# A rotation of 96 images by 90 degrees: the last 2 MB of loads in transfers of 48, 16 and 64 partitions instead of 64 and 64, and the first store released by the first of them

## The chip, the core and the metric

The kernel runs on one core of a Trainium2 chip. The metric is the device time of one execution in microseconds (us). Before the change it was 122.96 us, the median of 3 runs (122.85 to 123.09).

## What is computed

The input x is a float32 array of shape 32 x 3 x 256 x 256, 96 images of 256 x 256 and 25.17 MB in all. Each image is turned clockwise by 90 degrees:

```
def reference(x):
    return np.rot90(x, k=-1, axes=(-2, -1)).astype(np.float32)
```

So `out[.., i, j] = x[.., 255 - j, i]`. Nothing is added or multiplied. Each of the 25.17 MB is read from HBM once and written to HBM once, and between the two the elements change places on the chip.

## The kernel before, in words

**Tiling.** The 24,576 image rows are taken as 1,536 pieces of 16 rows (`R = 16`). A piece is 16 rows x 256 columns x 4 bytes = 16 KB and lies contiguously in HBM. Twelve pieces fall to each of the 128 partitions. They are cut into five groups (`sizes = (2, 2, 2, 4, 2)`, line 38), and each group has a tile of its own, `u0` to `u4`, with 2 or 4 pieces per partition. All twelve pieces of a partition are on the chip at once (192 KB), so no buffer is used a second time and no load waits for a buffer.

**Loads (lines 52 to 66).** All are issued by SyncE (SP). Group 0 comes in two transfers of 1 MB (line 55) and one of 2 MB (line 56). Groups 1 to 4 come in `I` = 2 or 4 transfers each (line 66): transfer `i` fills every `I`-th partition, starting at partition `i`. In groups 1, 2 and 4 this is 64 partitions with two pieces of 16 KB each, 2 MB per transfer. The last transfer of the last group is an exception (lines 62 to 64). It is cut by slot: line 63 loads slot 0 of partitions 1, 3, ..., 127 (64 pieces, 1 MB), and line 64 loads slot 1 of the same partitions (1 MB). Line 63's transfer is called `mark`.

**Turning (lines 68 to 101).** VectorE (DVE) does the turning with transposes of 32 x 32 blocks, 128 x 2048 elements per instruction. Since a transpose writes where another one has yet to read, one quarter or half of each group is parked in `spare` (in PSUM) or in `extra`, and ScalarE (ACT) copies it to its place afterwards (lines 78 and 98).

**Stores (lines 104 to 113).** They are issued by SP too, two per group, each from every second partition (`groups[n][a::2]`): eight of 2 MB and two of 4 MB (group 3). A store waits for the DVE and ACT instructions of its group. The very first store of group 0 (line 106, `a == 0`) has one dependency more, written by hand in lines 107 to 109: it waits until `mark` has landed. As SP issues in order, all the other stores stand behind it.

**What sets the order.** SP is one in-order queue: 14 loads, then 10 stores. The framework gives each DMA one of eight completion semaphores in turn. A DMA therefore waits, ahead of its issue, until the DMA eight places before it has landed, since both use the same semaphore. All transfers go through one DMA queue, which feeds the core's 16 DMA engines.

The list of transfers, with their places in SP's order:

| places | line | what | size of each |
|---|---|---|---|
| 0, 1 | 55 | group 0, slot 0 | 1 MB |
| 2 | 56 | group 0, slot 1 | 2 MB |
| 3 to 6 | 66 | groups 1 and 2 | 2 MB |
| 7 to 10 | 66 | group 3 | 2 MB |
| 11 | 66 | group 4, even partitions | 2 MB |
| 12 | 63 | group 4, odd partitions, slot 0 (`mark`) | 1 MB |
| 13 | 64 | group 4, odd partitions, slot 1 | 1 MB |
| 14, 15 | 106 | stores of group 0 | 2 MB |
| 16 to 19 | 113 | stores of groups 1 and 2 | 2 MB |
| 20, 21 | 113 | stores of group 3 | 4 MB |
| 22, 23 | 113 | stores of group 4 | 2 MB |

Of the kernel before, what the change touches and what calls it, by code (L numbers as in the profile page):

```python
# [1 line left out]

# [4 lines left out]


@with_exitstack  # L10
def kernel(
    ctx: ExitStack,
    tc: tile.TileContext,
    x: bass.AP,
    out: bass.AP,
):

    nc = tc.nc
    fp32 = mybir.dt.float32

    B, C, H, W = x.shape
    P = nc.NUM_PARTITIONS
    R = 16  # L30
    E = R * W
    hw = R // 2
    low, high = slice(0, hw), slice(hw, R)

    rows_in = x.rearrange("b c h w -> (b c h) w")
    rows_out = out.rearrange("b c h w -> (b c h) w")

    sizes = (2, 2, 2, 4, 2)
    first = [sum(sizes[:n]) for n in range(len(sizes))]
    groups = [  # L40
        ctx.enter_context(tc.tile_pool(name=f"group{n}", bufs=1)).tile([P, s, E], fp32, name=f"u{n}")
        for n, s in enumerate(sizes)
    ]
    psum = ctx.enter_context(tc.tile_pool(name="psum", bufs=1, space=bass.MemoryType.PSUM))
    spare = [psum.tile([P, E // 2], fp32, name=f"spare{h}") for h in range(2)]
    extra = ctx.enter_context(tc.tile_pool(name="extra", bufs=1)).tile([P, E // 2], fp32, name="extra")

    def rows_of(rows, n):
        return rows[first[n] * P * R : (first[n] + sizes[n]) * P * R]


    ld = rows_of(rows_in, 0).rearrange("(s i p r) w -> s i p (r w)", s=2, i=2, p=P)
    home = [groups[0][:, s].rearrange("p (i f) -> p i f", i=2) for s in range(2)]
    for i in range(2):
        nc.sync.dma_start(out=home[0][:, i], in_=ld[1, i])  # L55
    nc.sync.dma_start(out=home[1], in_=ld[0].transpose([1, 0, 2]))
    for n in range(1, len(sizes)):
        I = sizes[n]
        ld = rows_of(rows_in, n).rearrange("(a i m r) w -> i m a (r w)", a=2, i=I, m=P // I)
        to = groups[n].rearrange("p s f -> p (s f)").rearrange("p (a f) -> p a f", a=2)  # L60
        for i in range(I):
            if (n, i) == (len(sizes) - 1, I - 1):
                mark = nc.sync.dma_start(out=to[i::I, 0], in_=ld[i][:, 0])
                nc.sync.dma_start(out=to[i::I, 1], in_=ld[i][:, 1])
            else:
                nc.sync.dma_start(out=to[i::I], in_=ld[i])

    def turn_slab(src, dsts):
        s = src.rearrange("p (i r g c) -> p c r g i", i=2, r=R // 2, c=R)
        for h, d in enumerate(dsts):  # L70
            d = d.rearrange("p (c k r) -> p c r k", c=hw, r=R // 2)[:, :, ::-1, ::-1]
            nc.vector.transpose(out=d, in_=s[:, h * hw : (h + 1) * hw])  # L72

    u = groups[0]
    turn_slab(u[:, 0], spare)
    turn_slab(u[:, 1], [u[:, 0, : E // 2], u[:, 0, E // 2 :]])
    for h in range(2):
        nc.scalar.copy(out=u[:, 1, h * E // 2 : (h + 1) * E // 2], in_=spare[h])  # L78

    def turn_group(n, held):  # L80
        I = sizes[n]
        T = I // 2
        K = W // (R * T)
        u = groups[n].rearrange("p s f -> p (s f)")
        src = u.rearrange("p (a t r g c) -> p t c r g a", a=2, t=T, r=R, c=R)
        dst = u.rearrange("p (i c k t r) -> p t c r k i", i=I, c=R, k=K, t=T)[:, ::-1, :, ::-1, ::-1, :]
        for t in range(T):
            nc.vector.transpose(  # L88
                out=held[t].rearrange("p (i c k r) -> p c r k i", i=I, c=hw, k=K)[:, :, ::-1, ::-1, :],
                in_=src[:, t, low, low])  # L90
        for c, r in ((low, high), (high, high), (high, low)):
            for t in range(T):
                nc.vector.transpose(out=dst[:, t, c, r], in_=src[:, t, c, r])  # L93
        back = u.rearrange("p (i c k t r) -> p t i c k r", i=I, c=R, k=K, t=T)[:, ::-1]
        for t in range(T):
            kept = held[t].rearrange("p (i c k r) -> p i c k r", i=I, c=hw, k=K)
            for i in range(I):
                nc.scalar.copy(out=back[:, t, i, low, :, high], in_=kept[:, i])  # L98

    for n, held in enumerate(([extra], [spare[1]], spare, [extra]), 1):  # L100
        turn_group(n, held)


    st = rows_of(rows_out, 0).rearrange("(s i m r) w -> i m s (r w)", s=2, i=2, m=P // 2)
    for a in range(2):
        put = nc.sync.dma_start(out=st[a], in_=groups[0][a::2])
        if a == 0:
            tc.add_manual_dep(put.ins, mark.ins.name, mybir.DependencyInfo(
                mybir.DependencyClass.Sync, mybir.DependencyReason.SCHED_ONLY), reason="stores after loads")
    for n in range(1, len(sizes)):  # L110
        st = rows_of(rows_out, n).rearrange("(a i m r) w -> a m i (r w)", a=2, i=sizes[n], m=P // 2)
        for a in range(2):
            nc.sync.dma_start(out=st[a], in_=groups[n][a::2])


# [1 line left out]
_INS = ['x']  # L117
_OUTS = [((32, 3, 256, 256), 'float32')]


# [23 lines left out]
```

## Time and profile before

| what | value |
|---|---|
| median of 3 runs | 122.96 us (122.85 to 123.09) |
| the profiled execution's own time | 122.88 us |
| its span in the profile | 121.1 us |
| VectorE busy | 87.4 us (72%) |
| ScalarE busy | 14.9 us (12%) |
| DMA packets, bytes | 3456, 50.33 MB |
| HBM read, written | 25.17 MB, 25.17 MB |

The profile records one execution. The span is what it covers; the device time is 1.78 us more (122.88 - 121.1), which lies around the span. "Busy" counts an engine's own instructions. A DMA is issued by an instruction on SP's queue (SPq), which lasts about half a microsecond or more, and it lands, that is, its completion semaphore is full, much later. The profile also cuts time into stretches and gives, for each one, the share that the 16 DMA engines were at work and the GB/s. There a packet is booked whole in the stretch in which it starts, so short stretches can show shares over 1.

### The profile page before, as it was taken

The page shows a single profiled execution, that of the slowest core. Times are in us where ns is not written, and L with a number is a line of the kernel's source. Part 1 is how long each engine was busy: PE and PEld are TensorE (multiplying, and loading weights), DVE is VectorE, ACT ScalarE, POOL GpSimd, SP SyncE. Part 2 cuts the span into 40 slices and gives each one's busy share as a digit, 9 for nine tenths or more (in the row PEclk, how much of TensorE's full clock was granted, in tenths as well). Part 3 has the DMA queues.
Part 4 walks back from the last instruction along what each step waited for, and adds up shares of the span by engine and source line. Part 5 has one row for each costly group of instructions (what it writes and reads, how often), then busy time and mean ns, then how long its engine had stood idle before and what let it go on. Part 6 is the DMA issues. An engine that isn't in the chain of part 4 may idle for free.

```text
span 121.1 us, 131 instructions
## 1 busy us (share of the span) xinstructions
DVE 87.4 (72%) x24; ACT 14.9 (12%) x17; POOL 0.2 (0%) x4
## 2 busy tenths in 40 slices
DVE  0039999999999999999999999999999600000000
ACT  0000400380005100060000000318000330000000
POOL 0000000000000000000000000000000000000000
DMA  2999999999989898999999999999999999999994
GB/s 89 428 428 422 452 433 433 433 433 433 520 346 520 346 520 346 428 422 411 433 433 428 433 433 428 417 417 433 428 433 433 433 433 433 433 433 433 433 422 184
DMA packets 3456, 50.33 MB, mean 416 GB/s; under 512 B 384, under 2 KB 384, under 8 KB 384
## 3 DMA queue, kind: packets, MB, share of 16 engines
q1 hardware_dynamic: 3456, 50.33, 97.6%
HBM read 25.17 MB, written 25.17 MB: 416 GB/s over the span
## 4 chain that ended last, share of the span: by engine, by line
DVE 66%; issue 6%; DMA 6%; ACT 1%; ACTq 1%; SPq 0%; DVEq 0%
DVE u L93 39%; DVE spare L88 9%; DVE extra L88 6%; DVE u L72 6%; DVE spare L72 6%; DMA u<-in_x_dram 6%; ACT u L98 1%; ACTq L139 1%; SPq L55 0%; DVEq L88 0%; DVEq L72 0%
## 5 line engine op out<-in xcount | busy, mean ns | idle before, releaser
L93 DVE STREAM_TRANSPOSE u<-u 128x2048 f32<-128x2048 f32 x15 | 54.4, 3649 | 0.4
L72 DVE STREAM_TRANSPOSE spare<-u 128x2048 f32<-128x2048 f32 x2 | 7.1, 3586 | 8.1 <-DMA u<-in_x_dram 8.1
L98 ACT COPY u<-spare 128x512 f32<-128x512 f32 (+1 forms) x10 | 6.0, 687 | 38.5 <-DVE u L93 38.5
L88 DVE STREAM_TRANSPOSE spare<-u 128x2048 f32<-128x2048 f32 x3 | 10.7, 3588 | 0.0
L72 DVE STREAM_TRANSPOSE u<-u 128x2048 f32<-128x2048 f32 x2 | 7.8, 3988 | 0.0
L88 DVE STREAM_TRANSPOSE extra<-u 128x2048 f32<-128x2048 f32 x2 | 7.8, 3896 | 0.0
L98 ACT COPY u<-extra 128x1024 f32<-128x1024 f32 x4 | 4.0, 1043 | 22.8 <-DVE u L93 22.8
L78 ACT COPY u<-spare 128x2048 f32<-128x2048 f32 x2 | 3.6, 1870 | 8.7 <-DVE u L72 8.7
L78 ACT ACT_TABLE_LOAD x1 | 1.3, 1283 | 13.0 <-DMA u<-in_x_dram 13.0
L128 POOL MEMSET const-uint8-127<- 128x1 uint8 x1 | 0.1, 103 | 0.0
L128 POOL MEMSET const-bfloat16-1.0<- 128x1 bf16 x1 | 0.1, 102 | 0.0
L128 POOL MEMSET const-float32-0.0<- 128x1 f32 x1 | 0.1, 99 | 0.2 <-issue 0.2
L128 POOL MEMSET const-float32-1.0<- 128x1 f32 x1 | 0.1, 99 | 0.0
## 6 DMA issues: line engine op xcount, KB each, us to landing
u<-in_x_dram SPq DMA_DIRECT2D x10, 2048.0 KB, 30.4
out_dram<-u SPq DMA_DIRECT2D x8, 2048.0 KB, 18.2
out_dram<-u SPq DMA_DIRECT2D x2, 4096.0 KB, 21.1
u<-in_x_dram SPq DMA_DIRECT2D x4, 1024.0 KB, 20.5
```

Of the source, the lines that this page charges most:

```text
L72: nc.vector.transpose(out=d, in_=s[:, h * hw : (h + 1) * hw])
L78: nc.scalar.copy(out=u[:, 1, h * E // 2 : (h + 1) * E // 2], in_=spare[h])
L88: nc.vector.transpose(out=held[t].rearrange("p (i c k r) -> p c r k i", i=I, c=hw, k=K)[:, :, ::-1, ::-1, :], in_=src[:, t, low, low])
L93: nc.vector.transpose(out=dst[:, t, c, r], in_=src[:, t, c, r])
L98: nc.scalar.copy(out=back[:, t, i, low, :, high], in_=kept[:, i])
L128: nc = _bacc.Bacc("TRN2", target_bir_lowering=False, num_devices=1)
L139: with _tile.TileContext(nc) as tc:
```

## The change

The last transfer is cut into three instead of two. With `I = 2` and `P = 128`, `cut` is 3 x 128 / 8 = 48.

```
             if (n, i) == (len(sizes) - 1, I - 1):
-                mark = nc.sync.dma_start(out=to[i::I, 0], in_=ld[i][:, 0])
+                cut = 3 * P // (4 * I)
+                mark = nc.sync.dma_start(out=to[i : cut * I : I, 0], in_=ld[i][:cut, 0])
+                nc.sync.dma_start(out=to[cut * I + i :: I, 0], in_=ld[i][cut:, 0])
                 nc.sync.dma_start(out=to[i::I, 1], in_=ld[i][:, 1])
```

Slot 0 of the odd partitions now comes in two transfers: partitions 1 to 95 (48 pieces, 768 KB) and partitions 97 to 127 (16 pieces, 256 KB). Slot 1 comes as before (64 pieces, 1 MB). `mark` is now the transfer of 48, so the first store is held for that one alone. The pieces, their places and the order in which they are asked for stay the same. SP issues 15 loads instead of 14, and every later DMA moves on by one place, and by one semaphore of the eight. The instructions of DVE, ACT and the other engines and their order stay the same.

## The prediction

> **What bounds the kernel now.** I read the page first, engines and DMA rows together:
>
> ```profile
> span 121.1 us, 131 instructions
> DVE 87.4 (72%) x24; ACT 14.9 (12%) x17; POOL 0.2 (0%) x4
> DVE  0039999999999999999999999999999600000000
> DMA  2999999999989898999999999999999999999994
> q1 hardware_dynamic: 3456, 50.33, 97.6%
> DVE 66%; issue 6%; DMA 6%; ACT 1%; ACTq 1%; SPq 0%; DVEq 0%
> ```
>
> The chain of waits (last line) names DVE with 66%. That is a trap here. The DVE row is empty in the last eight slices, some 24 us, while the DMA row stands at 9 from the second slice to the last but one. The one DMA queue takes 97.6% of what 16 engines can give. The chain's last pieces are an ACT copy and a queue entry that end at 97.9 us; it does not follow the DMA data that drains until the end.
>
> The DMA row has 8s and 9s only, so I asked for stretches, cut at the places that matter: the start, the transfer of line 63, that of line 64, the first two stores, the end. Columns are the stretch, its length, DVE, ACT, POOL, clock, DMA share, GB/s.
>
> ```profile
> 0.00:1.70 1.70, 0.00 (x0) 0.00 (x0) 0.20 (x4) 1.00 0.00 0
> 1.70:119.90 118.20, 87.37 (x24) 14.93 (x17) 0.00 (x0) 1.00 1.00 426
> 119.90:121.10 1.20, 0.00 (x0) 0.00 (x0) 0.00 (x0) 1.00 0.00 0
> ```
>
> ```profile
> 56.00:58.50 2.50, 2.50 (x1) 0.00 (x0) 0.00 (x0) 1.00 0.99 419
> 58.50:61.00 2.50, 2.47 (x2) 0.00 (x0) 0.00 (x0) 1.00 0.99 419
> 61.00:66.00 5.00, 5.00 (x2) 0.00 (x0) 0.00 (x0) 1.00 1.04 446
> 66.00:71.00 5.00, 4.96 (x3) 0.00 (x0) 0.00 (x0) 1.00 1.03 442
> ```
>
> So the time is 1.70 us of start, 118.20 us in which all 16 DMA engines work without a hole, 1.20 us of end, and 1.78 us around the span: 122.88 us. The middle is 50.33 MB at 426 GB/s. Only three things can change the time: bytes, the pace of the engines, or a hole. The change keeps the bytes.
>
> Then I looked at the place of the change: SP's waits, the issues in time, and the times from issue to landing (of lines 63, 64 and 106, in this order).
>
> ```profile
> SPq L106 <- DMA u<-in_x_dram: 31.2, 1, 31.2
> SPq L64 <- DMA u<-in_x_dram: 4.4, 1, 4.4
> ```
>
> ```profile
> 22.75 0.51 SPq L63 DMA_DIRECT2D u<-in_x_dram  x1
> 27.64 0.49 SPq L64 DMA_DIRECT2D u<-in_x_dram  x1
> ```
>
> ```profile
> 59.43 1.37 SPq L106 DMA_DIRECT2D out_dram<-u  x2
> ```
>
> ```profile
> DMA to landing us min/median/max: 36.5/36.5/36.5
> ```
>
> ```profile
> DMA to landing us min/median/max: 34.1/34.1/34.1
> ```
>
> ```profile
> DMA to landing us min/median/max: 7.2/9.3/11.3
> ```
>
> `mark` lands at 22.75 + 36.5 = 59.25, and the first store is issued at 59.43. The longest wait of SP, 31.2 us, ends just there: this is the wait that the change shortens. But line 64's transfer lands only at 27.64 + 34.1 = 61.74. When the first store is issued, the engines still have most of line 64's 1 MB before them, 2.45 us of work at 428 GB/s. The first store lands at 59.43 + 7.2 = 66.6, the second at 60.1 + 11.3 = 71.4: 4.8 us apart, which is 2 MB at the queue's pace. If I go back one such step from the first landing, its data began at about 61.8 less the half microsecond or so by which landings trail the data, that is about 61.2, just where line 64's data ends. The stretches show the same: shares 0.99 and 1.04 on both sides of 61.00. The packet records agree: between 3 and 119 us no engine stands for over 0.04 us, the passage from loads to stores included.
>
> **The change, part by part.**
>
> *The release comes earlier.* 1 MB in 64 pieces takes 2.45 us, so each of 16 engines carries 4 pieces of 0.61 us. If the 48 pieces are 3 per engine, `mark` lands one piece sooner, at 59.25 - 0.61 = 58.64, and the first store is issued at about 58.82. It then has 2.2 us instead of 1.6 until the engines reach it at 61.0. The store's data cannot go ahead of line 64's in the one queue, so its first packet stays at 61.0. What is late next is not the wait but the queue itself. Gain: 0. The bounds: if all the idle time that the rounding of "1.00" allows (0.5% of 118.20 = 0.59 us) sat at this passage, the gain would be 0.59 us; the packet records speak for under 0.04. I take 0.
>
> *One DMA more.* Its issue costs SP about 0.50 us (line 63: 0.51). This lies at some 27.6 us, where SP then idles for 31 us, under a queue that holds over 30 us of data (landings 36.5 and 34.1 us after issue). Each further transfer ends on every engine with a small packet (384 under 512 bytes, 24 transfers x 16 engines). In the packet records it lasts 9 ns. The view's own bound is 0.59 us of idle time over 24 transfers, 0.025 us. I take +0.01.
>
> [...] The row: from line 63's transfer to line 64's the share is 0.99 and 0.99. [...]
>
> *The semaphores move on by one.* The last load now waits for the DMA in place 6 instead of 5. Lines 63 and 64 waited for two such loads, 4.89 us apart (22.75 and 27.64), so it is issued at about 27.64 + 4.9 = 32.5 us, and its data is due at 58.5: 26 us of cover. With that cover gone, each us of delay would be a hole of a us. The first store's semaphore was last used by place 7 instead of 6, a load of group 3 that lands over 20 us before 59. Stores in places 20 and 21 stand behind loads that land by 61.8, and are issued at 84.25. The last two stores wait for the same two stores as before, which land at 66.6 and 71.4, and are issued at 97.94. At 84.25 and 97.94 the queue still holds the earlier stores, so nothing comes late. DVE waits for one semaphore more ahead of group 4 (queue entries of this kind last about 0.02 us); it starts there at 81.04, 19 us after the loads. Cost: 0.
>
> *How the 48 and the 16 spread.* No row before has a transfer of 48 or of 16 pieces; the nearest are 64 pieces (line 63) and 32 of 32 KB (group 3), and both run at the full pace with 16 completions each. Bounds: 0 if they go 3 + 1 per engine, the sum of 4 that 64 pieces have now. If 48 pieces were cut as now, 4 to an engine, 12 engines would take them, and with one each of the 16 the fullest carries 5 instead of 4: +0.61 us. A gain is excluded, since 4 is the least maximum for 64 pieces over 16 engines. [...]
>
> *The 16 pieces lie in the last quarter of the partitions* (97 to 127), where 64 pieces lie across all. All rows of before span the partitions, so the price is open between 0 and one piece at half pace, again +0.61 us; below 0 nothing, as the pieces already go at the pace of the other rows. I take 0, by the nearest rows: whole partitions, every second, every fourth all ran at 419 to 446 GB/s.
>
> The sum is 122.88 + 0 + 0.01 = 122.89 us for the profiled execution, which is 0.08 us under the median of the runs, within their spread of 0.24. Against the median: **122.97 us**.
>
> **The rivals.** (0.2% is 0.25 us, about what a measurement of this kernel can tell from no change.)
>
> *A. No change*, 122.97. For it: the unbroken share, the landing of line 64 after the store's issue. Against it: nothing but what the trace cannot show, 48 and 16 pieces.
>
> *B. The fullest engine carries one piece more.* The place is the new pair of transfers, the price one piece, 0.61 us, for every further piece on one engine. All engines end within one piece of one another at 119.9, so an extra piece on any of them shows in full. It decides as soon as the 48 and 16 are not spread 3 and 1. Time: 122.97 + 0.61 = 123.58, slower. The neighbouring partitions would give the same size. For it: 48 is no power of two like all sizes before, and no row shows one. Against: 32, 64 and 128 pieces all use 16 engines.
>
> *C. The passage does have a hole when no profiler looks.* The first load took from its issue at 0.73 until 1.70 to reach an engine, 1.0 us, and the share in the next 1.1 us was only 0.58, so some engines started at about 2 us. A lead of 1.0 to 2.0 us for the first store, against 1.6 there is, would leave up to 0.4 us at some engines, and 0.6 more lead would remove it: 122.97 - 0.4 = 122.57. Against it: the profiled execution (122.88) has no hole and is as fast as the others (122.85 to 123.09).
>
> *D. The change doesn't do what it says*: the 48 land no sooner than the 64, because some engine still carries four of them. By itself that costs nothing: time 122.97 as in A, with the first store issued at 59.4 again.
>
> **How the numbers follow.** A with D 0.72, B 0.17, C 0.11. A's own spread is that of the runs, within 0.2%. So: faster 0.11, same 0.72, slower 0.17. The range takes A (122.75 to 123.2) and B (123.58) and leaves out C: 122.75 to 123.60.
>
> **What the profile after would show.** 3472 packets, 400 of them under 512 bytes (25 x 16); the last load issued at about 32.5; the first store at about 58.8 instead of 59.43; its landing still at about 66.6, now 7.8 us after its issue; the DMA share 1.00 from 1.70 to 119.90. B would show the last landing 0.6 us later with a share below 1.00 in the last 2 us; C an end below 119.9 with equal bytes. The forecast is wrong if the first store lands at another time than 66.6, or if the middle is not 118.2 us long.

## The result, and the profile after

The changed kernel takes **124.96 us** (median of 5 runs, 124.69 to 125.06), against 123.06 us for the kernel before (5 runs, 122.85 to 123.30): ratio 1.0153, 95% interval 1.0142 to 1.0164. It is 1.9 us slower, outside the forecast range of 122.75 to 123.60. The profiled execution took 124.69 us, 1.81 us more than that of before.

The page of the changed kernel:

```profile
span 122.9 us, 133 instructions
DVE 87.4 (71%) x24; ACT 14.9 (12%) x17; POOL 0.2 (0%) x4
DMA  3999999999998979799899999999999999999994
GB/s 85 427 427 427 437 443 432 432 443 437 448 501 352 512 341 512 341 427 341 256 427 427 427 427 427 427 427 427 427 427 427 427 427 443 459 448 427 443 427 171
DMA packets 3472, 50.33 MB, mean 410 GB/s; under 512 B 400, under 2 KB 400, under 8 KB 400
q1 hardware_dynamic: 3472, 50.33, 97.8%
```

DVE and ACT are what they were. The DMA row still shows 9s and a few 7s and 8s, and the queue's share is 97.8%, a little higher than before. Only the GB/s row tells what happened. In the slices of 3 us from the 12th to the 17th it swings between 341 and 512, about 427 on average, and the kernel before swings there in the same way (520, 346). But the 19th and 20th slices have 341 and 256 with no high slice beside them. The engines count as busy there (digits 9 and 8 of the DMA row) and move little.

The same in stretches, changed kernel first, then the kernel before. The last two columns are DMA share and GB/s:

```profile
1.70:56.20 54.50, 47.91 (x14) 8.84 (x7) 0.00 (x0) 1.00 1.00 424
56.20:61.20 5.00, 4.96 (x2) 0.00 (x0) 0.00 (x0) 1.00 0.99 249
61.20:121.70 60.50, 34.51 (x10) 6.10 (x10) 0.00 (x0) 1.00 1.00 429
```

```profile
1.70:56.20 54.50, 47.89 (x14) 8.84 (x7) 0.00 (x0) 1.00 1.00 425
56.20:61.20 5.00, 4.97 (x2) 0.00 (x0) 0.00 (x0) 1.00 1.02 433
61.20:119.90 58.70, 34.51 (x10) 6.10 (x10) 0.00 (x0) 1.00 1.00 426
```

Up to 56.2 us the two are alike. Then come the 48 and the 16 pieces, at 249 GB/s with a share of 0.99. In the packet records a piece of 16 KB takes 0.61 to 0.62 us before. In the changed kernel the 48 pieces run in three rounds of 16, with means of 0.81, 1.13 and 1.07 us; the 16 pieces take 1.10, and the first 16 pieces of the next transfer, slot 1, still take 0.99. Against 0.61 each, that is about 2.05 us more per engine. The first store's data begins at 63.11 us instead of 61.00: **+2.1 us**. After that the data goes a little faster, 429 instead of 426 GB/s: the stores' last packet ends 58.51 us after the first instead of 58.93, **-0.4 us**. The rest, 0.1 us, is the end of the execution.

The issues on SP's queue in the changed kernel, and line 64's time from issue to landing:

```profile
22.72 0.58 SPq L64 DMA_DIRECT2D u<-in_x_dram  x1
27.62 0.55 SPq L65 DMA_DIRECT2D u<-in_x_dram  x1
32.51 0.52 SPq L66 DMA_DIRECT2D u<-in_x_dram  x1
60.47 1.37 SPq L108 DMA_DIRECT2D out_dram<-u  x2
```

```profile
DMA to landing us min/median/max: 37.6/37.6/37.6
```

The last load is issued at 32.5 us and there are 3472 packets, as forecast. But `mark`, with fewer pieces, lands at 22.72 + 37.6 = 60.3 us, 1.1 us later than before instead of 0.6 sooner, and the first store goes out at 60.47. It lands 8.3 us later, at 68.8, where the prediction named any other time than 66.6 as a sign that it is wrong:

```profile
DMA to landing us min/median/max: 8.3/10.3/12.4
```

### The profile page after: what moved, and what is told of

Read it like the earlier page. It is cut to its first block, busy times and chain, and to the rows that moved or that the text cites. A ratio compares the mean times of both kernels' runs of the same rounds, so it can differ in the third digit from the quotient of the medians.

```text
span 122.9 us, 133 instructions
## 1 busy us (share of the span) xinstructions
DVE 87.4 (71%) x24; ACT 14.9 (12%) x17; POOL 0.2 (0%) x4
## 2 busy tenths in 40 slices
DMA packets 3472, 50.33 MB, mean 410 GB/s; under 512 B 400, under 2 KB 400, under 8 KB 400
## 3 DMA queue, kind: packets, MB, share of 16 engines
q1 hardware_dynamic: 3472, 50.33, 97.8%
## 4 chain that ended last, share of the span: by engine, by line
DVE 65%; issue 6%; DMA 5%; ACT 1%; ACTq 1%; SPq 0%; DVEq 0%
DVE u L95 39%; DVE spare L90 9%; DVE extra L90 6%; DVE u L74 6%; DVE spare L74 6%; DMA u<-in_x_dram 5%; ACT u L100 1%; ACTq L141 1%; SPq L55 0%; DVEq L90 0%; DVEq L74 0%
## 6 DMA issues: line engine op xcount, KB each, us to landing
u<-in_x_dram SPq DMA_DIRECT2D x1, 768.0 KB, 37.6
```

## The experiments

All times are medians beside the kernel before on the same chip, with the 95% interval of the ratio. The kernels q3, q4 and e12 put some rows of the output in other places and move the same bytes.

| run | how the last loads or stores are cut | us | ratio |
|---|---|---|---|
| q1 | slot 0 in 4 x 16: near partitions, near in HBM | 125.45 | 1.0204 (1.0189 to 1.0219) |
| q2 | 4 x 16: partitions 8 apart, 64 KB apart in HBM | 125.56 | 1.0207 (1.0192 to 1.0223) |
| q3 | 4 x 16: near partitions, 64 KB apart | 125.65 | 1.0211 (1.0188 to 1.0233) |
| q4 | 4 x 16: partitions 8 apart, near in HBM | 125.38 | 1.0201 (1.0186 to 1.0216) |
| e5 | slot 0 in 2 x 32: 1 to 63, 65 to 127 | 125.52 | 1.0204 (1.0187 to 1.0221) |
| e6 | slot 0 in 2 x 32: 1, 5, ... and 3, 7, ... | 122.78 | 0.9982 (0.9973 to 0.9991) |
| e7 | 2 x 64 by partitions: 1 to 63, 65 to 127 | 127.92 | 1.0400 (1.0385 to 1.0416) |
| e8 | 4 x 16, two of them over 33 to 95 | 124.24 | 1.0109 (1.0085 to 1.0132) |
| e9 | as before, release one load earlier | 123.15 | 1.0008 (0.9997 to 1.0019) |
| e10 | as before, release by the very last load | 125.40 | 1.0194 (1.0180 to 1.0208) |
| e11 | the kernel before | 123.00 | 1.0002 (0.9993 to 1.0011) |
| e12 | last stores by halves of the partitions | 132.93 | 1.0807 (1.0792 to 1.0821) |
| e13 | e6 again | 122.74 | 0.9983 (0.9971 to 0.9995) |
| e14 | e6, release by the second of the two | 123.05 | 1.0002 (0.9993 to 1.0011) |
| e15 | one more load, elsewhere, none narrower | 123.09 | 1.0004 (0.9995 to 1.0012) |

### Partitions, HBM addresses or size (q1 to q4)

The pieces were slow, but the packet records do not say why. Three theories: their partitions (P), their HBM addresses (H), or the size of the transfer (S). Slot 0 of the odd partitions was cut into four transfers of 16, in all four combinations of near and wide:

```
-                mark = nc.sync.dma_start(out=to[i::I, 0], in_=ld[i][:, 0])
+                for q in range(4):
+                    piece = nc.sync.dma_start(out=DST, in_=SRC)
+                    mark = piece if q == 2 else mark
 near DST: to[i + 32 * q : i + 32 * q + 31 : I, 0]     wide DST: to[i + I * q :: 4 * I, 0]
 near SRC: ld[i][16 * q : 16 * q + 16, 0]              wide SRC: ld[i][q::4, 0]
```

> Slot 0 of the odd partitions comes in four transfers of 16 pieces; transfer q takes 16 neighbouring odd partitions (32 of the 128) and 16 neighbouring pieces of HBM, so one piece per engine, 16 KB apart in HBM. The first store waits for the third. In the profile of the change the pieces of the 48 and the 16 took about 1.1 us instead of 0.61. Theory P (pieces that go to close partitions at the same time are slow): all four are slow, four pieces by 0.45 to 0.55, +1.8 to +2.2 us, 124.9 to 125.3. Theory H (pieces read at the same time from HBM addresses closer than the 64 KB that the engines are apart in the full-pace transfers are slow): the same, 124.9 to 125.3. Theory S (any small transfer is slow, wherever its pieces lie): the same or more. All three expect slow; this is the slow end that the next three are measured against.

> Four transfers of 16 pieces again, but transfer q takes every fourth odd partition (8 apart, across all 128) and every fourth piece of HBM (64 KB apart). Theory P: wide in the partitions, so full pace, 123.0 to 123.2. Theory H: wide in HBM, so full pace, 123.0 to 123.2. Theory S: slow as with the neighbouring ones, 124.9 or more.

> Four transfers of 16 pieces, to neighbouring partitions (32 of the 128) but from every fourth piece of HBM (64 KB apart). The pieces of slot 0 of the odd partitions change places with each other by this, so the output has rows in other places; bytes and instructions are those of the reference's work. Theory P: slow, 124.9 to 125.3. Theory H: full pace, 123.0 to 123.2. Theory S: slow.

> Four transfers of 16 pieces, to every fourth odd partition (across all 128) but from neighbouring pieces of HBM (16 KB apart). Here too the pieces of slot 0 of the odd partitions change places with each other. Theory P: full pace, 123.0 to 123.2. Theory H: slow, 124.9 to 125.3. Theory S: slow.

All four are slow by 2.4 to 2.7 us, about four pieces by 0.61. The stretches, of q1 and q2 in this order:

```profile
56.20:61.20 5.00, 4.97 (x2) 0.00 (x0) 0.00 (x0) 1.00 1.01 220
```

```profile
56.20:61.20 5.00, 4.96 (x2) 0.00 (x0) 0.00 (x0) 1.00 1.11 256
```

In the same stretch q3 has 210 GB/s and q4 249. P and H had both expected q2 to be fast, and both fell as I had drawn them. HBM addresses make no difference here: q3 differs from q1, and q4 from q2, in HBM alone, and they cost the same (125.65 and 125.45 us, 125.38 and 125.56). S held, but so did a form of P that I had not drawn: 16 partitions 8 apart may be no wider, for the DMA engines, than 16 neighbours.

### Size or partition groups (e5 to e8)

```
 e5: mark = to[1:64:2, 0] <- ld[i][:32, 0];   to[65::2, 0] <- ld[i][32:, 0];   then line 64 as before
 e6: mark = to[1::4, 0] <- ld[i][0::2, 0];    to[3::4, 0] <- ld[i][1::2, 0];   then line 64 as before
 e7: mark = to[1:64:2] <- ld[i][:32];         to[65::2] <- ld[i][32:]          (both slots; line 64 is gone)
 e8: to[33:94:4, 0] <- ld[i][16:47:2, 0];     to[35:96:4, 0] <- ld[i][17:48:2, 0];
     mark = to[1:32:2, 0] <- ld[i][:16, 0];   to[97::2, 0] <- ld[i][48:, 0];   then line 64 as before
```

> Slot 0 of the odd partitions in two transfers of 32 pieces: partitions 1 to 63, then 65 to 127. The four kernels with transfers of 16 pieces were all slow by 2.4 to 2.6 us, whether neighbouring or 8 partitions apart, so near and wide as I had drawn them do not decide. Two theories are left. Theory G (partition groups): what counts is how many groups of partitions the pieces in flight reach, and pieces within one half of the partitions reach half of the paths, so they go at half pace, 1.22 us instead of 0.61: four pieces per engine by 0.61, +2.4 us, 125.4, or less where engines get ahead into the other half. Theory S (size): a transfer under some size, here under 64 pieces, is slow whatever it touches: +2.4 us or, if only transfers of one piece per engine are slow, 0: 123.0 to 125.4. [...]

> Slot 0 of the odd partitions in two transfers of 32 pieces again, but interleaved: partitions 1, 5, ..., 125, then 3, 7, ..., 127. The same count of transfers and the same sizes as with the halves. Theory G: both reach all groups, as group 3's loads of every fourth partition do at full pace: 123.0, with `mark` (the first of the two) landing two pieces, 1.2 us, sooner than in the kernel before. Theory S: the same time as the halves.

> The last 2 MB in two transfers of 1 MB and 64 pieces each, as before, but cut by partitions instead of by slot: partitions 1 to 63 with both slots, then 65 to 127 with both slots. No transfer is smaller than before. Theory S: full pace, 123.0. Theory G: all eight pieces per engine are at half pace, 8 x 0.61 = +4.9 us, 127.8, less where engines get ahead into the other half.

> Slot 0 of the odd partitions in four transfers of 16 pieces: partitions 33, 37, ..., 93; then 35, 39, ..., 95; then 1, 3, ..., 31; then 97, 99, ..., 127. The first two take 16 pieces 4 apart across the middle of the partitions, the last two 16 neighbouring ones. Theory S: all four slow, 125.4 as in the four kernels before. Theory G: the first two at full pace (about 428 GB/s), the last two at half (about 215), so half of the 2.4 us: 124.2. [...]

Theory G is right in all four, to 0.2 us: 125.52 for 125.4, 122.78 for 123.0, 127.92 for 127.8, 124.24 for 124.2. That the halves of the partitions are its groups was the author's assumption before these runs. S falls twice. e5 and e6 have the same transfers by count and size and differ by 2.7 us; e7 has no transfer smaller and no transfer more than the kernel before and is the slowest. The stretches, of e5, e6 and e7 in this order:

```profile
56.20:61.20 5.00, 4.97 (x2) 0.00 (x0) 0.00 (x0) 1.00 1.12 246
```

```profile
56.20:61.20 5.00, 4.97 (x2) 0.00 (x0) 0.00 (x0) 1.00 1.00 426
```

```profile
56.20:66.00 9.80, 9.77 (x3) 0.00 (x0) 0.00 (x0) 1.00 1.05 231
66.00:72.00 6.00, 5.96 (x3) 0.00 (x0) 0.00 (x0) 1.00 0.95 404
```

In e7 the low pace fills the whole 9.8 us of its stretch, and the loss, 4.9 us, is twice that of e5 (2.5), for twice the bytes. e8 has both paces within one kernel, first the two transfers over 33 to 95, then the two of 16 neighbours:

```profile
55.50:57.40 1.90, 1.90 (x2) 0.00 (x0) 0.00 (x0) 1.00 1.00 414
57.40:60.40 3.00, 2.97 (x2) 0.00 (x0) 0.00 (x0) 1.00 1.01 251
60.40:64.00 3.60, 3.60 (x2) 0.00 (x0) 0.00 (x0) 1.00 1.03 437
```

Sixteen pieces, 256 KB, go at 414 GB/s when they lie 4 apart over the middle of the partitions, and at 251 (a stretch that also takes in a few faster packets at its ends) when they are neighbours. So 256 KB is not slow by its size: line 63's 1 MB goes at 419 GB/s before. HBM addresses changed along with the partitions in e5 to e8, but they do not order the times: q2's pieces lie 64 KB apart and go at 256 GB/s, e8's first two transfers have theirs 32 KB apart and go at 414.

Over all these runs, parts of one half of the partitions go at 210 to 246 GB/s (q1, q3, e5, e7), 16 partitions 8 apart at 249 to 256 (q2, q4), and 16 partitions 4 apart over 33 to 95 at full pace (e8, 414). The figures of q2, q4, e5 and e7 come with DMA shares of 1.05 to 1.12; divided by these they are 220 to 233, an estimate. Why these sets of partitions are slow, no run shows: the runs show which sets are. e8's transfers over 33 to 95 went at full pace without reaching over all 128 partitions.

### The release alone, and one more DMA alone (e9, e10, e11, e15)

```
 e9:  mark = the load of line 66 at place 11; lines 63 and 64 as before
 e10: mark = the load of line 64; every store waits for it
 e15: place 11 cut by slot into to[i::I, 0] and to[i::I, 1]; the rest as before
```

> The release alone: the loads stay as before (64 and 64 pieces), and the first store waits for the load before them (line 66, place 11), which lands some 2.4 us sooner than `mark` did. If the earlier release is worth nothing, because line 64's data fills the queue until 61.0 us: 122.98, the same as before. If the 0.2 us by which the interleaved transfers of 32 were under the kernel before come from their earlier release: 122.78 or less, since this one is earlier still.

> The other side of the release: loads as before, and all stores wait for the very last load (line 64), which lands at 61.74 us in the profile of before. From a DMA's issue to its first data the start of the kernel shows 1.0 us (0.73 to 1.70). So the queue should stand from 61.0 to about 62.9 or a little more: +1.9 to +2.5 us, 124.9 to 125.5. If the release had no such price, 123.0, and the lead of `mark` would be worth nothing.

> The kernel before, unchanged, against itself on this chip: it shows what differences mean nothing. Expected ratio 1.000 within 0.001. Its profile shows whether the pace of the stores after 72 us (613 to 616 ns per 16 KB in the first profile of before, 611 in those of the changed kernels) belongs to the kernel or to the execution.

> The kernel before with another load cut in two: group 4's even partitions come by slot, 64 pieces and 64 pieces, as the odd ones do. The last transfers and the release stay as before; all later DMAs move on by one semaphore. No transfer is narrower than before. If the shift makes the stores go faster: 0.998. If the shift does nothing: 1.000. Either way a further DMA by itself costs less than 0.1 us, not 2 us.

e9 gains nothing. e10 shows what the early release in the kernel before is worth: released by the last load, the queue stands for two microseconds, and the kernel takes 2.4 us more. Stretches of e10:

```profile
56.00:61.00 5.00, 4.96 (x2) 0.00 (x0) 0.00 (x0) 1.00 0.99 419
61.00:63.00 2.00, 2.00 (x2) 0.00 (x0) 0.00 (x0) 1.00 0.00 0
63.00:68.00 5.00, 4.97 (x3) 0.00 (x0) 0.00 (x0) 1.00 1.00 419
```

A hole looks like this: share 0.00, not 1.00 with few GB/s. e15 has the one DMA more of the change, and its shift of the semaphores, and costs 0.04% (interval -0.05% to 0.12%), at most 0.15 us. e11 says that 0.1% either way means nothing here.

### The small gain of the interleaved kernel (e13, e14)

e6 was 0.18% under the kernel before, and the changed kernel's own stores were faster. Were these chance, the release, or the shift by one DMA?

```
 e14: to[1::4, 0] <- ld[i][0::2, 0];    mark = to[3::4, 0] <- ld[i][1::2, 0];    then line 64 as before
```

> The interleaved two times 32 pieces again, unchanged, on whichever chip comes: if its 0.18% belong to the kernel, the ratio is again about 0.998 and the stores after 72 us go at 611 ns per 16 KB (429 GB/s); if they were that chip's or that hour's, the ratio is 1.000.

> The interleaved two times 32 pieces, with the first store held for the second of the two, which lands when `mark` of the kernel before does. If the small gain came from the earlier release: ratio 1.000. If it came from the DMA more, and so from the shift of all later DMAs by one semaphore: 0.998, as the interleaved kernel. If it is not the kernel's: 1.000 for all three of this call.

The gain repeats (0.9983) and it goes when the release moves to the second of the two (1.0002); the shift alone (e15) does not bring it. So it hangs on the release. Issue of the first store in e6, then in e14:

```profile
58.28 1.37 SPq L107 DMA_DIRECT2D out_dram<-u  x2
```

```profile
59.44 1.37 SPq L107 DMA_DIRECT2D out_dram<-u  x2
```

In neither is there a hole at 61: the DMA share from 56.2 to 61.2 us is 1.00 in e6 and 1.05 in e14, and after that 1.00 in both. What differs is the pace afterwards. This case has 17 profiles (e12 counts up to its last stores). In 11 of them the first store is issued 2.27 to 4.15 us ahead of its data (2.65 in the changed kernel, 2.7 in e6 and e13), and a store's piece takes 611 ns on average between 84 and 115 us. In the other six (before, e10, e11, e12, e14, e15) the lead is 1.33 to 1.60 us, and a piece takes 616 to 617 ns. No profile falls between. That is an association without exception, and e14 against e6 moves the release alone; but no run shows the mechanism. Nor is it the whole: e9 has the longest lead, 4.15 us, and its profiled execution took 122.81 us, yet its median is 123.15. Why the pace follows the lead, and what takes the gain from e9, stays open.

### Stores (e12)

```
-            nc.sync.dma_start(out=st[a], in_=groups[n][a::2])
+            rows = slice(64 * a, 64 * a + 64) if n == len(sizes) - 1 else slice(a, None, 2)
+            nc.sync.dma_start(out=st[a], in_=groups[n][rows])
```

> Does theory G hold for stores? The loads are as before; the last group's two stores take partitions 0 to 63 and 64 to 127 instead of every second one, so the rows of that group go to other places of the output. Bytes, sizes and waits are those of before. Theory G for reads of the partitions too: 16 pieces of 16 KB per engine at half pace, 16 x 0.61 = +9.8 us, 132.8. If only writes to the partitions are bound by it: 123.0.

132.93 us, for 132.8 expected. The HBM side of these stores is that of the kernel before, and only the partitions that each one reads differ. So a half of the partitions is slow to read from as well, 210 GB/s after 433 for the stores before, and HBM addresses have no part in it here:

```profile
90.00:110.00 20.00, 6.31 (x2) 1.99 (x2) 0.00 (x0) 1.00 1.02 433
110.00:130.00 20.00, 0.00 (x0) 0.00 (x0) 0.00 (x0) 1.00 0.97 210
```

## Why the prediction was wrong, point by point

**What bounds the kernel: right.** The one DMA queue does; 1.9 us of slower data became 1.9 us of time. Its three ways to change, "bytes, the pace of the engines, or a hole", were the right list. It then worked out the hole at length and gave the pace one short paragraph.

**The step that failed** is "The 16 pieces lie in the last quarter of the partitions". It was bounded by 0 and 0.61 us (half pace, an assumption that no row of before shows) and taken at 0, "by the nearest rows: whole partitions, every second, every fourth all ran at 419 to 446 GB/s". Those rows were near in step and far in what mattered: each of them crosses all 128 partitions. None of them could speak for a transfer that does not. The step was also drawn too small twice over. It asked about the 16 alone, though the 48 lie on partitions 1 to 95, two thirds of them in the lower half; and it priced one piece where the 3 of the 48, the 1 of the 16 and part of the first piece behind them are all slow. What the runs showed in its place: the 48 and the 16 both run slow (means of 0.81 to 1.13 us a piece instead of 0.61), and so does the first round behind them (0.99), +2.05 us in all; e5 against e6 shows that it lies in the partitions that they reach. With the whole of this in view, four pieces by 0.61, the upper bound would have been +2.4 us, and a range up to it would have held 124.96. e5 measures that bound (+2.5), the change itself +2.1.

**"How the 48 and the 16 spread": 3 + 1, as taken.** Before the change no run showed that; the changed kernel does. There are 400 small packets, 16 per transfer, and the pieces of the 48 follow one another in three rounds. Rival B had the right side, and named the neighbouring partitions, but only in an aside ("The neighbouring partitions would give the same size"); its main mechanism, an uneven share, did not occur. Nor did Rival D's, an engine with four of the 48, though its landing no sooner came true.

**"The release comes earlier": wrong in sign, and nearly right in price.** `mark` landed at 60.3 us instead of 58.64, since its own pieces were slow. No hole opened, as forecast, for slot 1's data was as late as everything else. The gain of 0 for an earlier release is nearly what e9 shows (1.0008); the stores' pace of e6, 0.2 us, was not foreseen, and Rival C, which had a gain of 0.4 from a hole, named another cause.

**"One DMA more", +0.01: not contradicted** (e15 allows up to 0.15), and here is a trap. The change has one DMA more and takes 1.9 us more, so the 1.9 us could be read as the price of a DMA. The runs say otherwise: e15 has one DMA more and stays within 0.15 us of before, e7 has none more and loses 4.9 us. A number that fits is no evidence for the rule that would explain it.

**"The semaphores move on by one", 0: right** (e15). The last load was issued at 32.51 for 32.5 forecast.

**Open:** why the 48 pieces go quite as slowly as they do. The packet records have 2.98 us from their first start to the start of the 16, against 1.83 us for the first three rounds of 16 pieces of line 63 in the kernel before. How pieces are dealt to engines was not measured. Nor did a run cut 48 and 16 pieces so that both reach over all the partitions; e6, with 32 and 32, stands in for it.

## What to carry to other kernels

When a transfer is cut, cut it by the free dimension, or by a small step of the partitions so that each part still reaches over all of them, and not by partition ranges: one more cut by the free dimension cost at most 0.15 us (e15), 32 + 32 by range cost 2.5 us, 32 + 32 interleaved (every fourth partition) nothing. Too large a step is no better than a range: every eighth partition was slow (q2 and q4, 256 and 249 GB/s). A DMA share of 1.00 says that the engines have work, not that they move it at full pace (0.99 with 249 GB/s in the changed kernel, 1.02 with 433 before); read the GB/s beside it. Before pricing an unseen operation by its nearest row, ask in which respects the rows of the trace are all alike, since the new one may differ in just that.

## What the runs showed of the hardware

- Transfers within one half of the partitions went at 210 to 246 GB/s instead of about 428 (line 64's transfer in the kernel before), as loads (16 partitions in q1 and q3, 32 in e5 and e7) and as stores (64 in e12).
- 16 partitions 8 apart over the whole range were as slow as 16 neighbours (q2 and q4, 125.56 and 125.38 us, against 125.45 and 125.65 in q1 and q3), while 16 partitions 4 apart over 33 to 95 went at full pace (e8, 414 GB/s). A wide span alone was not enough.
- Pieces behind such transfers took longer too: in the changed kernel the first 16 pieces of line 66, a transfer over all the partitions, took 0.99 us on average instead of 0.61.
- One DMA more in a full queue cost at most 0.15 us (e15, 2 MB cut into two of 1 MB), and two transfers of 256 KB went at 414 GB/s (e8), while a hole of 2 us in the queue (share 0.00 from 61 to 63 us) came back in full (e10, +2.4 us).
- With the first store issued 2.27 us or more ahead of its data, the later stores were 0.8% faster per piece (611 against 616 to 617 ns) than with 1.60 us or less, in all 17 profiles. This was not expected and is not explained.
